# A planner that orders a two-layer hybrid network: new costs, new priority shifts, first hidden blocks transposed on TensorE

## The chip, the cores and the metric

One Trainium2 chip, one NeuronCore of it. The metric is the time of one execution on the device, in microseconds, median of the runs. Engines are named as in the profile: PE is TensorE (PEld its weight loads), DVE is VectorE, ACT is ScalarE, POOL is GpSimd, SP is SyncE, which issues most of the transfers.

## What is computed

256 tokens of width 1024 go through six blocks: a gated feed-forward network (FFN), a hybrid mixer (gated delta rule beside a state-space scan), an FFN, an FFN, a sparse-attention mixer (NSA), an FFN. After each block the residual is scaled, added and layer-normed. All in float32. What matters here:

```
def swiglu(x, w_in, w_out):
    gate, up = jnp.split(x @ w_in, 2, axis=-1)
    return (jax.nn.silu(gate) * up) @ w_out          # D_MODEL 1024, D_FF 2816

proj = x @ w_in                                       # hybrid mixer: 1024 -> 5664 columns
o_a, o_b = gdn_branch(...), ssd_branch(...)           # 64-token chunks with a triangular solve; 128-token chunks
return jnp.concatenate([o_a, o_b], axis=-1) @ w_out

proj = x @ w_in                                       # NSA: 16 heads, compressed + selected + window attention
return o @ w_out
```

## The kernel before

**Numbers.** TensorE's full-rate float32 type rounds its operands, so every operand is split in two: `hi` is a rounded copy (`whi<-raw`, mostly on ACT) and `lo` is the rest (`wlo<-raw,whi`, a subtraction on DVE). A product is hi·hi + hi·lo + lo·hi, three matmuls (`mm3`, `split`). So each 512 KB tile of weights (`raw`, 128x1024) costs one transfer, one ACT instruction and one DVE instruction before its matmuls.

**FFN blocks.** The 2816 hidden columns are 22 blocks of 128 (`ffn`, L1274 on). In FFN 2, 3 and 4 the first four blocks are made by `small(b)` (L1339) for each half b of 128 tokens, tokens on partitions: matmuls into a `ps` bank, silu on ACT, product on DVE (`sg`). The second matmul needs them with hidden columns on partitions, so they are turned. `S_TURN` (L117) says how, one entry for each FFN and half: 0 is four PE transposes into an `mp` bank (`mp<-ident,sg`), read from there by `split`; 1 is `turn` (L793): ACT takes the float words apart (`words<-sg`), SP issues a transposing transfer (`turned<-words`), ACT puts the words together (`gT<-turned`). FFN 1 does not use `S_TURN`. The other blocks come in groups of four by a seven-product scheme (`wide`, L945) with sums of weight tiles on DVE (`raw<-raw,raw`) or by POOL transfers that add (POOLq `raw<-in_ffn_w_in_dram`), or singly (`ordinary`). `term` adds each finished block into four `acc` banks.

**Banks.** PSUM has 2 banks under the name `ps`, 2 under `mp` and 4 under `acc` (`CAPS`). `mp` takes the transposes of layer norm, of `small` with S_TURN 0, and products of `wide`.

**The order of work.** Nothing is emitted as written. `K` records every instruction with its dependencies in a `Plan`; `Plan.order` (L481) then runs a list scheduler over five engines. An instruction's priority is its place in the program plus a shift from the table `SHIFTS` (L51): for each block and engine, runs of (count, shift). `price` (L396) says what an instruction costs, `LAT` what a hand-over between two engines costs, and `Rings` (L259) when a transfer lands, from two queues (SP and POOL) that share the bandwidth. What comes out is a fixed order for each engine, and each engine keeps to it: an instruction that waits holds up all behind it on its engine. All emission goes through one line, so every row of the profile has L682; rows are told apart by tiles.

Of the kernel before, what the change touches and what calls it, by code (L numbers as in the profile page):

```python
# [43 lines left out]

SHARE = {"tensor": 1.0}

# [6 lines left out]
        "tensor": [(54, 312), (4, 0), (5, 633), (69, 0), (5, -34), (66, 1525), (75, 578)],  # L53
        "vector": [(26, 0), (10, -363), (1, 0), (2, -172), (4, 0), (16, -136), (12, 0), (1, 159), (9, 0), (1, 199), (1, 0), (8, 70), (3, 121),
            (29, 0), (70, -36)],
        "scalar": [(100, 156), (13, 0), (2, 210)],
        "sync": [(8, 0), (2, -433), (2, -185), (1, -325), (1, 0), (2, -185)],
    },
    1: {
        "tensor": [(78, 97), (43, 0), (2, -396), (28, 0), (3, 84), (20, -93), (49, 2), (3, -168), (50, 0), (1, 71), (63, 0), (1, 591), (16, 0),  # L60
# [4 lines left out]
        "vector": [(63, 0), (21, -37), (19, 176), (54, 0), (2, 370), (17, 0), (1, 364), (31, 0), (3, 471), (18, 144), (7, 0), (6, -279), (2, 382),  # L65
            (51, -379), (5, 136), (68, 0), (23, -449)],
        "scalar": [(73, 0), (3, -1527), (2, 92), (36, 0), (1, 444), (84, 0), (25, -178), (5, 174), (5, 0), (1, 92)],
    },
    2: {
        "tensor": [(43, 277), (1, 0), (3, 89), (43, 0), (8, 217), (14, 0), (2, 189), (26, 0), (1, -988), (266, 0), (1, 1556), (4, 0), (2, 1846),  # L70
            (84, 1283), (37, 0), (5, 1492), (7, 1066), (51, 661), (9, 306), (69, 0), (74, -484), (25, 0), (3, -165)],
        "vector": [(37, 382), (25, 303), (16, 0), (1, 336), (10, 0), (1, 407), (25, 0), (2, 1164), (2, 0), (4, 853), (2, 0), (1, 880), (4, 16),
            (6, 0), (6, 1372), (30, 0), (8, 391)],
        "scalar": [(120, 177)],
    },
    3: {
        "tensor": [(54, 860), (19, 0), (2, 765), (29, 432), (13, 0), (13, 277), (2, 424), (29, 0), (4, 114), (9, 402), (2, 590), (53, 0), (7, 303),
            (1, 264), (126, 0), (6, 1322), (23, 959), (31, 445), (221, 32), (120, 0), (24, 459)],
        "vector": [(8, 0), (81, 492), (1, -170), (2, 0), (95, -215)],
        "scalar": [(35, 0), (1, 556), (71, 0), (7, -444)],  # L80
    },
    4: {
        "tensor": [(37, 330), (25, 0), (9, -331), (233, 0), (131, -65), (2, 141), (14, 0), (6, 80), (28, 0), (4, 349)],
        "vector": [(25, 0), (1, 42), (42, 0), (3, -385), (71, 0), (1, -281), (7, 0), (1, -271)],
        "scalar": [(91, 0), (8, -135), (27, 0), (2, -179), (11, 0), (2, 344), (70, 0), (1, -358), (2, -304), (3, 108)],
        "gpsimd": [(64, 67)],
        "sync": [(2, 0), (41, -12)],
    },
    5: {
        "tensor": [(113, 0), (14, 265), (47, 0), (15, -122), (47, 239), (12, 0), (108, 365), (12, 0), (8, -4893), (69, 0), (10, 46), (8, 0),  # L90
            (11, 181), (7, 0), (3, 239), (4, 0), (15, 405), (31, 0), (2, 110), (24, 0), (1, 292), (41, 0), (179, -266)],
        "vector": [(21, 0), (26, -366), (83, 0), (1, -97), (3, 0), (3, -70), (47, -356)],
        "scalar": [(43, 0), (7, -108), (64, -148), (17, 226)],
# [23 lines left out]
S_TURN = (0, 1, 1, 1, 0, 1, 0, 1)  # L117
# [136 lines left out]
class Op:  # L254
    __slots__ = ("eng", "fn", "args", "kw", "idx", "prio", "cost", "table", "deps", "succ", "ndep", "ready", "start",
                 "end", "alloc", "dense", "alts", "tiles", "nbytes", "quad", "port", "banks", "pad")


class Rings:  # L259


    LEAD = dict(sync=1500.0, gpsimd=2200.0)
    TAIL = dict(sync=1600.0, gpsimd=4300.0)
    START = 20000.0
    SHARE = dict(sync=0.52, gpsimd=0.48)
# [5 lines left out]
    def advance(self, to):  # L271
        while self.now < to:
            open_ = [e for e in self.left if self.left[e]]
            if not open_:
                self.now = to
                return
            rate = {e: self.SHARE[e] if len(open_) > 1 else 1.0 for e in open_}
            step = min([to - self.now] + [self.left[e][0] / rate[e] for e in open_])
            for e in open_:
                self.left[e][0] -= rate[e] * step  # L280
                if self.left[e][0] < 1e-6:
                    self.left[e].pop(0)
            self.now += step if step > 1e-9 else 1e-9

    def landing(self, eng, at, nbytes, row):
        if eng == "gpsimd":
            work = nbytes / 217.0
        else:
            work = max(150.0, nbytes / (359.0 if row >= 4096 else 341.0 if row >= 2048 else 310.0 if row >= 1024 else
                                        267.0 if row >= 512 else 200.0))  # L290
        if at < self.START:
            work *= 1.07
        at += self.LEAD[eng]
        self.advance(at)
        self.left[eng].append(work)
        other = "sync" if eng == "gpsimd" else "gpsimd"
        mine, more = sum(self.left[eng]), sum(self.left[other])
        a, b = self.SHARE[eng], self.SHARE[other]
        took = mine / a if mine / a <= more / b else more + mine
        return max(self.now, at) + took + (600.0 if at < self.START else self.TAIL[eng])  # L300


class Plan:
# [5 lines left out]
           "vector": dict(tensor=202.0, vector=127.0, scalar=165.0, gpsimd=155.0, sync=120.0),  # L309
           "scalar": dict(tensor=217.0, vector=152.0, scalar=131.0, gpsimd=170.0, sync=150.0),  # L310
           "gpsimd": dict(tensor=203.0, vector=100.0, scalar=150.0, gpsimd=112.0, sync=150.0)}
# [84 lines left out]
    def price(self, op, eng, fn, args, kw):  # L396
# [15 lines left out]
        if fn in DMAS:  # L412
            return 455.0 if eng == "sync" else 1300.0
# [4 lines left out]
        if eng == "scalar":  # L418
            rows = args[0].p1 - args[0].p0

            more = 0
# [55 lines left out]
    TURN = 150.0  # L477
    TABLES = {"Exp": "exp", "Silu": "silu", "Sin": "silu"}


    def order(self, caps):  # L481
        ops = self.ops
        for op in ops:
# [4 lines left out]
            op.ready = 0.0  # L488
            for d in op.deps:
                ops[d].succ.append(op)  # L490
# [35 lines left out]
        def try_alloc(key):  # L526
            q = queues[key]
            while heads[key] < len(q):
# [18 lines left out]
                for op in wait:  # L547
                    op.alloc.remove(t)
                    op.ready = max(op.ready, t.slot_free)
                    if not op.alloc:  # L550
                        release_ready(op)
# [9 lines left out]
        def deps_done(op):  # L561
            for t in list(op.alloc or []):
                if t.slot_free is not None:
                    op.alloc.remove(t)
                    op.ready = max(op.ready, t.slot_free)
            if op.alloc:
# [10 lines left out]
        while left:  # L577
# [42 lines left out]
            if eng == "tensor":  # L620
                partial = op.quad
                l, r = args[1:3]
# [13 lines left out]
            if fn in DMAS:  # L636

                v = args[0] if isinstance(args[0], V) else args[1]
                op.end = rings.landing(e, st, op.nbytes, 256 if fn != "dma_start" else 4 * v.shape[-1])
                free[e] = st + c  # L640
# [8 lines left out]
            for s in op.succ:  # L649
                lat = (620.0 if s.eng == "gpsimd" and s.fn == "dma_start" else 80.0) if fn in DMAS else self.latency(op, eng, s.eng) + (0.0 if eng == "tensor" else s.pad)  # L650
                s.ready = max(s.ready, op.end + lat)
                s.ndep -= 1
# [1898 lines left out]
```

## Time and profile before

| what | value |
|---|---|
| median of 3 runs (lowest, highest) | 1077.56 us (1076.8, 1080.67) |
| the profiled execution | 1073.77 us |
| its span, first to last instruction | 1072.1 us |
| granted TensorE clock, mean over the span | 0.994 |
| PE busy | 1049.2 us, 98% |
| DVE busy | 1006.0 us, 94% |
| ACT busy | 773.7 us, 72% |
| POOL busy | 87.5 us, 8% |
| DMA, mean | 219 GB/s |

Busy time of PE counts a matmul from its issue to the modelled end of its pipeline, and matmuls overlap. So PE can be "busy" and still not at its pace: the pace is the distance between starts. Along the blocks: FFN 1 runs to about 190 us, the hybrid mixer to 420, FFN 2 to 600, FFN 3 to 780, NSA to 895, FFN 4 to the end.

### The profile page before, as it was taken

To read this page: it belongs to the slowest core of one execution; us is meant where nothing else is said; L and a number is where in the kernel's file an instruction comes from. 1 tells how busy PE (TensorE), PEld (TensorE's weight loads), DVE (VectorE), ACT (ScalarE), POOL (GpSimd) and SP (SyncE) were. 2 spreads that over 40 slices of the span, in tenths; PEclk is the share of its full clock that TensorE was granted. 3 is DMA by queue.
4 is the path that set the end of the run, shared out by engine and by line. 5 is a ranking of instruction groups with operands and counts; after the bars stand their busy time and mean duration, and the time that the engine had idled before them with its cause. 6 is when DMAs were issued, how large, how long until landed. Compare 5 with 4: busy or idle time off the path is not lost. (4 is left out here: it accounts for less than half of the span.)

```text
span 1072.1 us, 15945 instructions
## 1 busy us (share of the span) xinstructions
PE 1049.2 (98%) x5698; PEld 868.7 (81%) x5698; DVE 1006.0 (94%) x1413; ACT 773.7 (72%) x1158; POOL 87.5 (8%) x136
## 2 busy tenths in 40 slices
PE   9999999999999999999999999999999999999997
PEld 7877788898889877888878887788887778888886
DVE  7998999898998989899999999999988989999997
ACT  7666876479866966778767486797566975878790
POOL 1001000001000111010000200000021101000100
PEclk9999999999999999999999999999999999999999
DMA  9888996745772689799879857788744346498991
GB/s 328 279 251 267 272 282 202 220 115 148 175 207 71 196 272 302 199 270 286 258 212 312 221 164 232 225 290 239 257 149 172 101 156 177 134 271 236 285 282 40
DMA packets 182809, 234.56 MB, mean 219 GB/s; under 512 B 51197, under 2 KB 112330, under 8 KB 182730
## 3 DMA queue, kind: packets, MB, share of 16 engines
q1 hardware_dynamic: 173482, 215.72, 63.8%
q0 software_dynamic: 9248, 17.83, 9.5%
q8 instruction: 45, 0.74, 0.3%
q14 instruction: 34, 0.28, 0.1%
HBM read 221.30 MB, written 1.07 MB: 207 GB/s over the span
## 5 line engine op out<-in xcount | busy, mean ns | idle before, releaser
L682 DVE TENSOR_TENSOR wlo<-raw,whi 128x1024 fp32r<-128x1024 f32 (+2 forms) x447 | 522.4, 1208 | 9.2 <-ACT whi L682 9.0
L682 ACT ACTIVATE whi<-raw 128x1024 fp32r<-128x1024 f32 (+2 forms) x430 | 426.8, 1044 | 69.9 <-DVE raw L682 51.4
L682 PE MATMUL ps<-whi,x 128*128 128x512 f32 (+1 forms) x544 | 143.6, 384 | 0.0
L682 DVE TENSOR_TENSOR raw<-raw,raw 128x1024 f32<-128x1024 f32 x94 | 112.2, 1219 | 4.7 <-DMA raw<-in_ffn_w_in_dram 4.5
L682 PEld LDWEIGHTS ps<-whi,x 128*128 128x128 f32 x544 | 97.9, 188 | 17.9 <-ACT vg L682 0.2
L682 PE MATMUL ps<-x,whi 128*128 128x256 f32 (+2 forms) x464 | 105.0, 342 | 0.1
L682 PE MATMUL acc<-wlo,gh 128*128 128x512 f32 x253 | 99.0, 391 | 0.1
L682 PE MATMUL acc<-whi,gl 128*128 128x512 f32 x253 | 98.0, 391 | 0.0
L682 PE MATMUL acc<-whi,gh 128*128 128x512 f32 x253 | 96.8, 392 | 0.0
L682 PEld LDWEIGHTS ps<-x,whi 128*128 128x128 f32 (+1 forms) x464 | 77.7, 188 | 10.1 <-ACT cv L682 0.6
L682 PE MATMUL acc<-whi,x 128*128 128x512 f32 x256 | 82.5, 403 | 2.8 <-ACT x L682 1.2
L682 PE MATMUL mp<-whi,x 128*128 128x512 f32 x288 | 78.6, 395 | 0.3 <-ACT vg L682 0.3
L682 PE MATMUL ps<-wlo,x 128*128 128x512 f32 (+1 forms) x272 | 77.8, 383 | 0.6 <-DVE wlo L682 0.6
L682 PE MATMUL mp<-whi,fhi 128*128 128x512 f32 x192 | 75.6, 394 | 0.0
L682 PE MATMUL mp<-whi,flo 128*128 128x512 f32 x192 | 75.4, 393 | 0.0
L682 POOL DMA_DIRECT2D raw<-in_ffn_w_in_dram x34 | 41.1, 1219 | 347.2 <-PE mp L682 171.1
L682 PE MATMUL ps<-x,wlo 128*128 128x256 f32 (+1 forms) x344 | 67.6, 286 | 0.0
L682 PEld LDWEIGHTS mp<-whi,x 128*128 128x128 f32 x288 | 53.9, 190 | 12.9 <-ACT vg L682 1.1
L682 PE MATMUL acc<-whi,g 128*128 128x512 f32 x192 | 63.3, 390 | 0.0
L682 PE MATMUL mp<-wlo,fhi 128*128 128x512 f32 x192 | 60.3, 394 | 2.8 <-DVE wlo L682 2.6
L682 PEld LDWEIGHTS acc<-whi,x 128*128 128x128 f32 x256 | 47.2, 188 | 14.7 <-DVE x L682 2.3
L682 PEld LDWEIGHTS ps<-wlo,x 128*128 128x128 f32 x272 | 49.2, 188 | 9.7 <-DVE wlo L682 1.1
(330 smaller groups left out, 1853.6 us busy)
## 6 DMA issues: line engine op xcount, KB each, us to landing
raw<-in_ffn_w_in_dram SPq DMA_DIRECT2D x162, 512.0 KB, 6.0
raw<-in_ffn_w_out_dram SPq DMA_DIRECT2D x88, 512.0 KB, 5.9
raw<-in_hyb_w_in_dram SPq DMA_DIRECT2D x44, 512.0 KB, 5.3
raw<-in_ffn_w_in_dram POOLq DMA_DIRECT2D x34, 512.0 KB, 8.4
raw<-in_ffn_w_in_dram SPq DMA_DIRECT2D x52, 256.0 KB, 4.4
raw<-in_hyb_w_out_dram SPq DMA_DIRECT2D x16, 512.0 KB, 4.6
raw<-in_nsa_w_in_dram SPq DMA_DIRECT2D x10, 512.0 KB, 5.3
raw<-in_nsa_cmp_w_dram SPq DMA_DIRECT2D x8, 512.0 KB, 3.9
```

Source lines behind the costliest of these rows:

```text
L682: r = getattr(getattr(nc, eng), fn)(*[res(a) for a in args], **{k: res(a) for k, a in kw.items()})
```

## The change

1. `S_TURN` becomes all 0: four halves (both of FFN 2, the second of FFN 3 and of FFN 4) leave the transposing transfer and take the PE transposes.
2. The planner's costs change: issue of a transposing transfer on SP 1350 instead of 455 ns, of any other 500; a weight load that finds no cover adds up to 109 ns to a matmul; hand-overs to PE get shorter (so that this is not counted twice); a transposing transfer that meets one of POOL's costs 1500 ns more; bandwidths, lead and tail of a landing are new; SP stands still when its queue is deep.
3. Every entry of `SHIFTS` is new (more runs per engine; tables for SP in blocks where there were none).

```diff
-S_TURN = (0, 1, 1, 1, 0, 1, 0, 1)
+S_TURN = (0, 0, 0, 0, 0, 0, 0, 0)
 class Rings:
-    LEAD = dict(sync=1500.0, gpsimd=2200.0)
-    TAIL = dict(sync=1600.0, gpsimd=4300.0)
+    LEAD = dict(sync=1400.0, gpsimd=2570.0)
+    TAIL = dict(sync=2000.0, gpsimd=3300.0)
-    SHARE = dict(sync=0.52, gpsimd=0.48)
+    SHARE = dict(sync=0.43, gpsimd=0.57)
+    CLASH = 1500.0
+    DEEP = 9200.0
...
+        if (turning and self.left[other]) or (eng == "gpsimd" and any(t for _, t in self.left[other])):
+            work += self.CLASH
...
-           "vector": dict(tensor=202.0, vector=127.0, scalar=165.0, gpsimd=155.0, sync=120.0),
-           "scalar": dict(tensor=217.0, vector=152.0, scalar=131.0, gpsimd=170.0, sync=150.0),
+           "vector": dict(tensor=140.0, vector=127.0, scalar=165.0, gpsimd=155.0, sync=120.0),
+           "scalar": dict(tensor=155.0, vector=152.0, scalar=131.0, gpsimd=170.0, sync=150.0),
...
-            return 455.0 if eng == "sync" else 1300.0
+            return 1300.0 if eng == "gpsimd" else 500.0 if fn == "dma_start" else 1350.0
...
+                slack = free[e] - op.rel
+                if slack < self.LOAD:
+                    c += min(self.LOAD, self.LOAD - slack)
+                elif 200.0 <= slack < 240.0:
+                    c += 60.0
...
-                free[e] = st + c
+                free[e] = st + c + (max(0.0, rings.deep - rings.DEEP) if e == "sync" else 0.0)
...
 SHIFTS = {
     0: {
-        "tensor": [(54, 312), (4, 0), (5, 633), (69, 0), (5, -34), (66, 1525), (75, 578)],
+        "tensor": [(73, 35), (42, 0), (3, -303), (2, 677), (60, 285), (4, 0), (6, 272), (80, 180), (61, 0), (1, 89), (2, 0), (5, 76), (12, 0),
...
```

In numbers of instructions: PE gets 16 transposes more (`mp<-ident,sg` 16 to 32, one row of the profile each). ACT loses 4 `words<-sg`, 4 `gT<-turned`, and gets 2 more table loads (15 to 17); SP loses 4 transposing transfers (36 to 32); 8 pairs `g<-gT` become `g<-mp`. Copies that may run on either engine are dealt anew: DVE gets 4 `whi<-raw` more (16 to 20) and gives 4 `PT<-mp` to ACT; 8 small products go from POOL to DVE. All else is the same work in another order.

**PE near 100 us (FFN 1).** The two transposes `mp<-ident,vg` and `mp<-ident,su` turn a finished group of four blocks; both use the two `mp` banks. Before:

```order
228 L682 MATMUL mp_198_1159<-ident_7_285,vg_129_836 128x128 x4
229 L682 MATMUL acc_112_778<-wlo_181_1084,g_94_680 128x512
230 L682 MATMUL acc_112_778<-whi_178_1069,g_94_680 128x512
231 L682 MATMUL acc_114_784<-whi_178_1069,g_94_680 128x512
232 L682 MATMUL acc_114_784<-wlo_181_1084,g_94_680 128x512
233 L682 MATMUL acc_114_784<-whi_178_1069,g_94_680 128x512
234 L682 MATMUL acc_118_795<-whi_178_1069,g_94_680 128x512
235 L682 MATMUL acc_118_795<-wlo_181_1084,g_94_680 128x512
236 L682 MATMUL acc_118_795<-whi_178_1069,g_94_680 128x512
237 L682 MATMUL mp_207_1189<-ident_7_285,su_102_729 128x128 x4
```

Now:

```order
238 L707 MATMUL acc_101_707<-whi_171_1031,g_113_773 128x512
239 L707 MATMUL acc_101_707<-wlo_180_1068,g_113_773 128x512
240 L707 MATMUL acc_101_707<-whi_171_1031,g_113_773 128x512
241 L707 MATMUL acc_101_707<-whi_175_1048,g_113_773 128x512
242 L707 MATMUL acc_101_707<-wlo_182_1078,g_113_773 128x512
243 L707 MATMUL acc_101_707<-whi_175_1048,g_113_773 128x512
244 L707 MATMUL acc_114_776<-whi_203_1175,gh_205_1184 128x512
245 L707 MATMUL acc_114_776<-wlo_206_1188,gh_205_1184 128x512
246 L707 MATMUL acc_116_784<-whi_203_1175,gh_205_1184 128x512
247 L707 MATMUL acc_116_784<-wlo_206_1188,gh_205_1184 128x512
248 L707 MATMUL mp_212_1208<-ident_7_284,su_90_653 128x128 x4
```

The `vg` transposes are row 234 now, so 13 matmuls (rows 235 to 247) stand between the two, where 8 stood.

**DVE near 541 us (FFN 2).** `raw<-raw,raw` adds weight tiles that have just landed; `wlo<-raw,whi`, `su` and `vg` work on what is there already. Before:

```order
684 L682 TENSOR_TENSOR wlo_1020_5639<-raw_991_5533,whi_1015_5624 128x1024
685 L682 TENSOR_TENSOR wlo_1023_5649<-raw_994_5544,whi_1019_5637 128x1024
686 L682 TENSOR_TENSOR raw_1010_5610<-raw_1010_5610,raw_1013_5616 128x1024
687 L682 TENSOR_TENSOR wlo_1027_5668<-raw_1002_5574,whi_1025_5658 128x1024
688 L682 TENSOR_TENSOR raw_1012_5614<-raw_1012_5614,raw_1014_5618 128x1024
689 L682 TENSOR_TENSOR su_980_5494<-mp_968_5423,su_980_5494 128x512
690 L682 TENSOR_TENSOR wlo_1031_5691<-raw_1005_5585,whi_1028_5675 128x1024
```

Now:

```order
691 L707 TENSOR_TENSOR wlo_1015_5626<-raw_989_5518,whi_1011_5606 128x1024
692 L707 TENSOR_TENSOR wlo_1020_5641<-raw_993_5531,whi_1014_5623 128x1024
693 L707 TENSOR_TENSOR su_984_5502<-mp_974_5461,su_984_5502 128x512
694 L707 TENSOR_TENSOR wlo_1025_5658<-raw_995_5540,whi_1019_5639 128x1024
695 L707 TENSOR_TENSOR vg_980_5487<-vg_980_5487,su_984_5502 128x512
696 L707 TENSOR_TENSOR wlo_1029_5675<-raw_998_5551,whi_1023_5650 128x1024
697 L707 TENSOR_TENSOR wlo_1032_5687<-raw_1002_5566,whi_1026_5661 128x1024
698 L707 TENSOR_TENSOR wlo_1034_5697<-raw_1005_5577,whi_1031_5680 128x1024
699 L707 TENSOR_TENSOR raw_1010_5601<-raw_1010_5601,raw_1017_5630 128x1024
```

Row 686 of before is row 699 now: six instructions that stood behind it (`su`, `vg` and four `wlo`) stand ahead of it.

**PE at the start of FFN 2.** `mp<-ident,sg` are the transposes that came in; `ps_782`, `ps_807` and `ps_822` are banks in which other products are summed meanwhile. Now (before, no transposes stood in this stretch of matmuls):

```order
1271 L707 MATMUL ps_807_4671<-whi_757_4433,x_780_4537 128x512 x2
1272 L707 MATMUL ps_782_4549<-wlo_801_4635,x_780_4537 128x512
1273 L707 MATMUL ps_782_4549<-wlo_804_4649,x_780_4537 128x512 x2
1274 L707 MATMUL mp_809_4685<-ident_7_284,sg_799_4624 128x128 x2
1275 L707 MATMUL ps_807_4671<-whi_757_4433,x_780_4537 128x512 x2
1276 L707 MATMUL ps_807_4671<-whi_770_4485,x_780_4537 128x512 x4
1277 L707 MATMUL ps_807_4671<-whi_772_4494,x_780_4537 128x512
1278 L707 MATMUL mp_814_4705<-ident_7_284,sg_811_4690 128x128 x2
1279 L707 MATMUL ps_807_4671<-whi_772_4494,x_780_4537 128x512 x3
```

Two transposes each stand between matmuls of another bank. Elsewhere, near 380 us: on SP the last `G<-rates` transfer of the hybrid mixer moves ahead of two of the `w_out` loads that stood before it; on PE the eight matmuls `mp<-xdt,G` that use it stand 9 matmuls earlier (a place in the order 2075, was 2084). Near 805 us (NSA): `PT<-mp`, a copy out of an `mp` bank, is on ACT right after the softmax; it was on DVE behind ten other instructions.

## Rows read from the trace of the kernel before

**Rows 1.** The page, part 1 (busy time of each engine, share of the span, instructions) and part 2 (PE's granted clock in 40 slices, tenths):

```profile
PE 1049.2 (98%) x5698; PEld 868.7 (81%) x5698; DVE 1006.0 (94%) x1413; ACT 773.7 (72%) x1158; POOL 87.5 (8%) x136
...
PEclk9999999999999999999999999999999999999999
```

**Rows 2.** The busy time of the engines in stretches of 20 us (stretch, length, then PE, PEld, DVE, ACT, POOL busy, granted clock, DMA share, GB/s):

```profile
60.00:80.00 20.00, 17.69 (x72) 13.85 (x71) 17.38 (x18) 11.79 (x13) 2.39 (x2) 0.93 0.79 222
...
480.00:500.00 20.00, 20.00 (x90) 16.27 (x89) 20.00 (x19) 18.24 (x21) 0.00 (x0) 1.00 0.99 311
```

**Rows 3.** PE's own waits (engine and tile that waited, on whom, us in total, times, longest), the first four and the last of 15 rows that sum to 14.8 us:

```profile
PE mp L682 <- DVE wlo L682: 2.6, 2, 2.3
PE mp L682 <- DVE G L682: 1.9, 1, 1.9
PE mp L682 <- DVE PT L682: 1.5, 1, 1.5
PE mp L682 <- DVE gl L682: 1.5, 1, 1.5
...
PE mp L682 <- DVE y L682: 0.2, 1, 0.2
```

**Rows 4.** Groups of PE instructions by tile and shape (count | busy us, mean ns of one | idle before, releasers):

```profile
L682 PE MATMUL ps<-whi,x 128*128 128x512 f32 x480 | 133.4, 395 | 0.0
L682 PE MATMUL acc<-whi,x 128*128 128x512 f32 x256 | 82.5, 403 | 2.8 <-ACT x L682 1.2 <-ACT whi L682 1.0 <-DVE x L682 0.6
L682 PE MATMUL acc<-whi,g 128*128 128x512 f32 x192 | 63.3, 390 | 0.0
L682 PE MATMUL ps<-x,whi 128*128 128x512 f32 x224 | 61.0, 403 | 0.1
L682 PE MATMUL acc<-wlo,x 128*128 128x512 f32 x128 | 48.4, 401 | 0.0
L682 PE MATMUL mp<-ident,sg 128*128 128x128 f32 x16 | 2.6, 272 | 0.0
```

**Rows 5.** Timeline (start us, length us, engine, instruction, [idle before <- what ended it]): four matmuls of 512 columns, and four transposes of `sg`, on PE at full pace:

```profile
620.06 1.09 PE L682 MATMUL mp<-whi,x 128*128 128x512 f32 x4
...
618.35 0.60 PE L682 MATMUL mp<-ident,sg 128*128 128x128 f32 x4
```

**Rows 6.** What the transposing path costs its engines: groups on ACT (count | busy, mean ns), and the transfer's issue on SP (count: ns min/median/max):

```profile
L682 ACT ACTIVATE words<-sg 128x1024 uint16<-128x1024 uint16 x4 | 4.2, 1052 | 2.6 <-DVE sg L682 2.6
...
L682 ACT ACTIVATE gT<-turned 128x1024 uint16<-128x1024 uint16 x24 | 32.9, 1369 | 4.0 <-DMA turned<-words 4.0
L682 ACT ACT_TABLE_LOAD x15 | 19.2, 1283 | 1.0 <-PEq L2538 0.8
...
L682 SPq DMA_TRANSPOSE turned<-words x36: 1231/1239/5765, 100.7 to 1016.9; - x36
```

**Rows 7.** Timeline of the waits that this text follows, in order of time:

```profile
98.16 1.06 ACT L682 ACTIVATE whi<-raw 128x1024 fp32r<-128x1024 f32 x1 [1.70 <-DMA raw<-in_ffn_w_out_dram]
...
100.48 0.66 PE L682 MATMUL mp<-ident,su 128*128 128x128 f32 x4 [1.47 <-DVE gl L682]
...
375.98 4.27 SPq L682 DMA_DIRECT2D raw<-in_hyb_w_out_dram  x3
381.90 0.33 SPq L682 DMA_DIRECT2D G<-rates  x1
...
389.31 2.45 ACT L682 ACTIVATE G<-G,arena 128x128 f32<-128x128 f32 x8 [3.48 <-DMA G<-rates]
...
394.93 0.29 PE L682 MATMUL mp<-xdt,G 128*128 128x64 f32 x1 [1.88 <-DVE G L682]
...
412.52 0.50 PE L682 MATMUL acc<-whi,x 128*128 128x512 f32 x1 [1.15 <-ACT x L682]
...
414.31 0.73 PE L682 MATMUL acc<-whi,x 128*128 128x512 f32 x2 [0.60 <-DVE x L682]
...
542.07 1.23 DVE L682 TENSOR_TENSOR raw<-raw,raw 128x1024 f32<-128x1024 f32 x1 [1.86 <-DMA raw<-in_ffn_w_in_dram]
...
547.36 0.74 PE L682 MATMUL ps<-wlo,x 128*128 128x512 f32 x2 [0.63 <-DVE wlo L682]
...
550.78 0.50 PE L682 MATMUL ps<-whi,fhi 128*128 128x512 f32 x1 [0.59 <-ACT whi L682]
...
805.63 0.55 PE L682 MATMUL mp<-ident,P 128*128 128x128 f32 x3 [1.52 <-DVE PT L682]
```

**Rows 8.** Timeline of waits whose surroundings stay as they are or get no more room (72 to 78 us, and 665 us):

```profile
72.91 2.36 DVE L682 TENSOR_TENSOR raw<-raw,raw 128x1024 f32<-128x1024 f32 x2 [2.45 <-DMA raw<-in_ffn_w_in_dram]
...
76.46 0.73 PE L682 MATMUL mp<-wlo,fhi 128*128 128x512 f32 x2 [2.31 <-DVE wlo L682]
...
77.72 0.63 PE L682 MATMUL mp<-whi,fhi 128*128 128x512 f32 x1
78.14 0.63 PE L682 MATMUL mp<-whi,flo 128*128 128x512 f32 x1
...
665.01 0.50 PE L682 MATMUL acc<-wlo,g 128*128 128x512 f32 x1 [0.87 <-DVE wlo L682]
```

**Rows 9.** How long an `mp` bank is held after a pair of transposes of `sg` (600 to 660 us; instruction, count: ns min/median/max, first and last start):

```profile
L682 ACT ACTIVATE g<-mp x2: 377/384/391, 618.8 to 619.1; 128x256 fp32r<-128x256 f32 x2
L682 DVE TENSOR_TENSOR g<-mp,g x2: 415/416/417, 619.3 to 619.6; 128x256 fp32r<-128x256 f32 x2
```

More of the change, by code (lines that the diff above doesn't have):

```diff
@@ L69 @@
-    2: {
[L70 to L74, printed above, removed]
-    },
@@ L277, in advance, with landing @@
             rate = {e: self.SHARE[e] if len(open_) > 1 else 1.0 for e in open_}
-            step = min([to - self.now] + [self.left[e][0] / rate[e] for e in open_])
+            step = min([to - self.now] + [self.left[e][0][0] / rate[e] for e in open_])
             for e in open_:
-                self.left[e][0] -= rate[e] * step
-                if self.left[e][0] < 1e-6:
+                self.left[e][0][0] -= rate[e] * step
+                if self.left[e][0][0] < 1e-6:
                     self.left[e].pop(0)
             self.now += step if step > 1e-9 else 1e-9
-    def landing(self, eng, at, nbytes, row):
+    def landing(self, eng, at, nbytes, row, turning):
         if eng == "gpsimd":
-            work = nbytes / 217.0
+            work = nbytes / 224.0
         else:
[L289 to L292, printed above, removed]
+            work = max(185.0, nbytes / (365.0 if row >= 4096 else 330.0 if row >= 2048 else 305.0 if row >= 1024 else
+                                        281.0 if row >= 512 else 225.0))
+        early = at < self.START
         at += self.LEAD[eng]
         self.advance(at)
-        self.left[eng].append(work)
         other = "sync" if eng == "gpsimd" else "gpsimd"
-        mine, more = sum(self.left[eng]), sum(self.left[other])
+        if (turning and self.left[other]) or (eng == "gpsimd" and any(t for _, t in self.left[other])):
+            work += self.CLASH
+        self.left[eng].append([work, turning])
+        mine, more = sum(w for w, _ in self.left[eng]), sum(w for w, _ in self.left[other])
         a, b = self.SHARE[eng], self.SHARE[other]
         took = mine / a if mine / a <= more / b else more + mine
-        return max(self.now, at) + took + (600.0 if at < self.START else self.TAIL[eng])
+        self.deep = mine
+        return max(self.now, at) + took + self.TAIL[eng]
 class Plan:
@@ L477 @@
     TURN = 150.0
+    LOAD = 109.0
     TABLES = {"Exp": "exp", "Silu": "silu", "Sin": "silu"}
@@ L488, in order @@
             op.ready = 0.0
+            op.rel = -1e9
             for d in op.deps:
@@ L565, in deps_done @@
                     op.ready = max(op.ready, t.slot_free)
+                    op.rel = max(op.rel, t.slot_free)
             if op.alloc:
@@ L638, in order @@
                 v = args[0] if isinstance(args[0], V) else args[1]
-                op.end = rings.landing(e, st, op.nbytes, 256 if fn != "dma_start" else 4 * v.shape[-1])
-                free[e] = st + c
+                op.end = rings.landing(e, st, op.nbytes, 256 if fn != "dma_start" else 4 * v.shape[-1], fn != "dma_start")
+                free[e] = st + c + (max(0.0, rings.deep - rings.DEEP) if e == "sync" else 0.0)
             else:
@@ L651, in order @@
                 s.ready = max(s.ready, op.end + lat)
+                if eng != "tensor":
+                    s.rel = max(s.rel, op.end + lat)
                 s.ndep -= 1
```

62 lines of the change are left out of this document (39 added, 23 removed), and 8 rows, old and new, of the table SHIFTS.

## The prediction

> **What bounds the kernel now.** I read the page's busy shares first. PE is busy for 98% of the span at a granted clock of nearly full speed in every slice, DVE for 94%, ACT for 72% [rows 1]. In an FFN stretch (480 to 500 us) PE and DVE both fill 20.00 of 20 us [rows 2]. So I looked next at what PE waits for: 15 rows that sum to 14.8 us of 1072.1, the largest 2.6 us [rows 3]. The reader is to see that PE hardly ever stands idle for long: over 98% of the span is made of instructions one behind the other, and nothing that only relieves another engine can shorten it. A change of order can take time from three places alone: PE's listed waits; the small excess between neighbours, which the waits do not list; and the work itself.
>
> The small excess shows in the means by group. A matmul of 512 columns reads 390 ns where nothing disturbs it (`acc<-whi,g`), and four in a row take 1.09 us, so their starts lie (1.09 − 0.39)/3 = 0.23 us apart [rows 4, 5]. Other groups of the same shape read 395 to 403 ns. The records of neighbours overlap; the difference to 390 is the part that waited for weights or for a bank.
>
> **Work added and removed.** PE gets 16 transposes. Four take 0.60 us and one record reads 272 ns, so each behind another costs (0.60 − 0.27)/3 = 0.11 us, and 16 cost 1.8 us [rows 4, 5]. They stand in pairs between matmuls of other banks, where the next one starts as it would have; if each stood alone they would cost 16 × 0.272 = 4.4 us. I take 1.8, since the order shows them in pairs, and keep 4.4 as the upper bound.
> The Trainium skill ("TensorE: Matmul & The Clock Gate", Part 4: PE-mode transpose) gives about 275 ns for a 128×128 transpose in one kernel's context; by it the estimate would be 16 × 275 ns = 4.4 us and the whole sum 2.6 us longer. The trace agrees on the length of one record (272 ns) and not on the pace of several.
>
> The transposing path that goes takes from ACT four `words` of 1.05 us and four `gT` of 1.37 us, and adds two table loads of 1.28 us: 9.7 − 2.6 = 7.1 us less. From SP it takes four issues of 1.24 us [rows 6]. ACT is busy for 72% [rows 1], and no listed wait of PE hangs on these, so both count nothing; they are covered by PE's own work of about 98%. If that cover were gone, the most they could give is their length, which I do not add. Eight pairs `g<-gT` become `g<-mp`, one ACT and one DVE instruction as before, 0.38 and 0.42 us [rows 9]; DVE gets four copies more and gives four away. Nothing is counted for these: DVE's work stays within 1 us of its 1006, and it has 66 us of idle time over the span [rows 1].
>
> **Waits that lose their cause.** I followed each long wait of PE to its root [rows 7] and looked where the instructions stand now.
> - 100.48, 1.47 us: ACT waited 1.70 us for a `w_out` load, was late with the product that DVE needed, and PE had only 8 matmuls to cover. Now 13 stand there: 5 × 0.23 = 1.2 us more cover. I credit 1.2.
> - 394.93, 1.88 us: ACT waited 3.48 us for the transfer `G<-rates`, which SP issued at 381.90, behind three `w_out` loads that took 4.27 us to issue. It now goes ahead of two of them, about two thirds of 4.27 us earlier (2.8 us). But PE needs it 9 matmuls, or 2.1 us, earlier. The gain to be had lies between 0 and 1.88; since its issue moves by more than its use, and the transfer has less ahead of it on the queue, I take all 1.88.
> - 414.31, 0.60 us: five `wlo` stood in front of the layer norm's DVE steps and are behind them now. Credit 0.6. The 1.15 us at 412.52 belong to a transfer that landed late, and stay.
> - 547.36 and 550.78, 0.63 and 0.59 us: DVE stood 1.86 us at 542.07 for a tile that had not landed, with `su` and four `wlo` ready behind it. Six ready instructions stand ahead of it now. At the 1.2 us of one such instruction that is far more than 1.86 us. Credit 1.2.
> - 805.63, 1.52 us: the copy `PT` stood on DVE behind ten others; it is on ACT right after the softmax. Credit 1.5.
>
> Together 1.2 + 1.9 + 0.6 + 1.2 + 1.5 = 6.4 us. Bounds: nothing, if each gap comes back somewhere else; 11.0 us, if every wait shown goes (these 6.4, the rest of 100.48, 412.52, and the two of [rows 8]).
>
> **Kept.** The wait at 76.46, 2.31 us, comes from DVE standing 2.45 us for a transfer; the order of these loads and of DVE around it is as before. Behind it matmuls of 0.63 us start 0.42 us apart, at half the clock [rows 8], where 0.23 is usual: some eight of them lose 8 × 0.19 = 1.5 us, and the granted clock of that stretch is 0.93 [rows 2]. This can go only with the wait, so I count it at nothing and keep 1.5 us for the lower bound. At 665.01 the cover shrinks by about 1.4 us; the 0.87 us stay.
>
> **The small excess.** The planner now charges up to 109 ns for a weight load without cover, so it will choose neighbours that cover it. What there is to gain, against 390 ns: 13 × 256 + 13 × 224 + 5 × 480 + 11 × 128 ns = 3.3 + 2.9 + 2.4 + 1.4 = 10.0 us [rows 4]. Between 0 and 10.0 I take a third, 3.3 us: the list scheduler can only choose among what is ready, and the priorities bind it first.
>
> **The sum.** The profiled execution took 1073.8 us. 1073.8 + 1.8 − 6.4 − 3.3 = 1065.9. The median of the three runs is 1077.56, so the profiled execution stands 3.8 us below it; on the median's scale the forecast is 1065.9 + 3.8 = 1069.7, say 1070 us. Lowest: all waits, the clock and all excess go, and only the transposes are added: 1073.8 + 1.8 − 11.0 − 1.5 − 10.0 + 3.8 = 1057. Highest, with the mechanism as I see it but nothing credited and the transposes dear: 1073.8 + 4.4 + 3.8 = 1082.
>
> **The rivals.** What a measurement of this kernel can tell from no change is about 0.5%, 5.4 us.
> - *More goes than I credit.* The loads of FFN 2, 3 and 4 stand some 4 us of PE's work earlier relative to their use in the new order, so also transfers that I left alone may land in time. For: most roots above are transfers that landed late, and their times are what the planner was corrected in. Against: at 480 to 500 us the transfer engines are already 99% taken at 311 GB/s [rows 2], and an earlier issue does not land earlier there. Time: 1056 to 1062.
> - *The waits only change places.* Six blocks in a new order have hundreds of new hand-overs, and none shown by the old trace says that those are met. For: DVE too is full in FFN stretches [rows 2], so what PE gains it would soon wait for there; the order cannot then beat the 20 us of DVE. Against: PE's waits on DVE come to a few us in all [rows 3]. The order would not do what it says, and only the transposes remain: 1077.6 + 1.8 = 1079.4.
> The Trainium skill ("Perfetto Trace Analysis", Identifying the Most-Contended Engine) has TensorE's headroom judged by its weight loads' busy share rather than its matmuls'. By that PE is at 81% here and DVE, at 94%, is the engine to relieve; as the change relieves DVE of nothing, this rival would be the result. The waits in the trace speak against it: an engine that bounds would be waited for by more than 14.8 us.
> - *Slower: the two `mp` banks get scarce.* Each new pair of transposes takes an `mp` bank until DVE has read it. From 618.35, when the transposes begin, to 619.3 + 0.42 = 619.7, when the first pair is read, is 1.4 us [rows 5, 9]. Products of the seven-product scheme and the transposes of the layer norm want the same two banks. If PE has less than 1.4 us of other ready work at each of the eight, it stands for 8 × 1.4 = 11.2 us: 1077.6 + 1.8 + 11.2 = 1090.6. It decides from about 0.5 us of work per pair downwards (8 × 0.9 = 7.2 us). Against it: at the start of FFN 2 the order has seven matmuls of another bank, 1.6 us, between the first two pairs.
>
> **How the numbers follow.** The forecast has a chance of 0.50; its spread, 1062 to 1077, puts 0.36 below 1072.2 and 0.14 above. The larger gain has 0.17, all faster. Waits that change places have 0.20, 0.17 of it within 0.5% and 0.03 beyond. The scarce banks have 0.13, beyond. So faster is 0.36 + 0.17 = 0.53, same 0.14 + 0.17 = 0.31, slower 0.03 + 0.13 = 0.16. The range 1056 to 1083 holds the first three cases and leaves out the scarce banks and a little at each end. The likeliest case's own range, 1062 to 1077, is nearly all at or below the time before.
>
> **What the profile after would show.** Right: `mp<-ident,sg` x32 at about 272 ns with no idle time before it; PE's waits summing to some 8 to 9 us; none of 1 us or more before the transposes of `su` near 100 us, before `mp<-xdt,G`, before the matmuls fed by `raw<-raw,raw` near 545 us, or before the transposes of `P` in NSA; `acc<-whi,x` and `ps<-x,whi` below 400 ns; the wait near 76 us still there. Wrong: the same sum of waits at other tiles (waits that change places); idle time before `mp` tiles on ACT's or DVE's `g` (scarce banks); DVE waiting for `raw` longer than before; or a time below 1062 with the group means unchanged, which would mean that I misjudged where PE loses time.

## The result, and the profile after

The changed kernel takes **1069.6 us** (median of 8 runs, 1066.65 to 1073.53); the kernel before took 1076.44 us (8 runs). The ratio is 0.9935, 95% interval [0.9912, 0.9958]. The forecast was 1070 us. In a second comparison the ratio was 0.9921 [0.9900, 0.9943]. The profiled execution took 1069.88 us, its span is 1068.2 us, 3.9 us less than the span before.

The page, part 1, to be held against [rows 1]:

```profile
PE 1051.2 (98%) x5714; PEld 869.8 (81%) x5714; DVE 1004.6 (94%) x1417; ACT 765.7 (72%) x1154; POOL 88.5 (8%) x130
```

PE has its 16 instructions more and is as full as before, ACT lost 8 us of work, and the time fell by less than 1%. The shares of busy time say nothing of the gain. PE's own waits do (on whom, us in total, times, longest), all of them, against the 14.8 us in [rows 3]:

```profile
PE acc L707 <- ACT whi L707: 2.6, 2, 1.5
PE mp L707 <- DVE wlo L707: 1.8, 2, 1.4
PE acc L707 <- DVE wlo L707: 1.7, 2, 0.9
PE acc L707 <- POOL ones L707: 1.1, 1, 1.1
PE acc L707 <- issue: 0.6, 1, 0.6
PE mp L707 <- ACT P L707: 0.6, 2, 0.3
PE ps L707 <- ACT cv L707: 0.5, 2, 0.2
PE mp L707 <- DVE arena L707: 0.4, 1, 0.4
PE mp L707 <- DVE h L707: 0.2, 1, 0.2
```

They sum to 9.5 us; 8 to 9 were forecast. `G`, `PT`, `gl`, `x` and the two `ps` waits for weights have left the list. The timeline of PE shows the place near 100 us and what is left (start, length, instruction, [idle before <- what ended it]):

```profile
76.64 0.73 PE L707 MATMUL mp<-wlo,fhi 128*128 128x512 f32 x2 [1.38 <-DVE wlo L707]
...
96.60 0.60 PE L707 MATMUL mp<-ident,vg 128*128 128x128 f32 x4
...
100.04 0.60 PE L707 MATMUL mp<-ident,su 128*128 128x128 f32 x4
...
798.23 0.66 PE L707 MATMUL mp<-ident,P 128*128 128x128 f32 x4 [0.36 <-DVE arena L707]
...
1021.72 0.50 PE L707 MATMUL acc<-whi,gh 128*128 128x512 f32 x1 [1.51 <-ACT whi L707]
1022.98 0.50 PE L707 MATMUL acc<-wlo,gh 128*128 128x512 f32 x1 [0.76 <-DVE wlo L707]
...
1029.71 0.50 PE L707 MATMUL acc<-wlo,gh 128*128 128x512 f32 x1 [0.94 <-DVE wlo L707]
```

Before `su` there is no idle time now. The three waits in FFN 4 are new, 3.2 us together. In this trace they lead back to ACT and SP (SPq is SP's issue of transfers):

```profile
1002.30 9.73 SPq L707 DMA_TRANSPOSE turned<-words  x2
1012.13 11.56 SPq L707 DMA_DIRECT2D raw<-in_ffn_w_out_dram  x10
...
1020.62 1.06 ACT L707 ACTIVATE whi<-raw 128x1024 fp32r<-128x1024 f32 x1 [3.06 <-DMA raw<-in_ffn_w_out_dram]
```

Two transposing transfers took 9.73 us to issue, so the `w_out` loads behind them were issued from 1012.13 on, and ACT stood 3.06 us for the first. Each of the 32 such transfers takes 1.28 us in the middle case, but up to 6.09 (before 1.24 and 5.77, [rows 6]):

```profile
L707 SPq DMA_TRANSPOSE turned<-words x32: 1232/1284/6093, 95.8 to 1008.5; - x32
```

The groups of PE that answer to [rows 4]:

```profile
L707 PE MATMUL ps<-whi,x 128*128 128x512 f32 x480 | 136.2, 397 | 0.0
...
L707 PE MATMUL acc<-whi,x 128*128 128x512 f32 x256 | 82.2, 404 | 1.1 <-ACT whi L707 1.1
...
L707 PE MATMUL ps<-x,whi 128*128 128x512 f32 x224 | 62.0, 408 | 0.0
...
L707 PE MATMUL acc<-wlo,x 128*128 128x512 f32 x128 | 47.5, 396 | 0.0
...
L707 PE MATMUL mp<-ident,sg 128*128 128x128 f32 x32 | 5.7, 273 | 0.0
```

The 32 transposes have no idle time before them. The means that were to fall did not: 397, 404, 408 against 395, 403, 403; only `acc<-wlo,x` fell, 401 to 396.

### The profile page after: what moved, and what is told of

It reads as the page before. It is cut to its first block, busy times and chain, and to the rows that moved or that the text cites. A ratio compares the mean times of both kernels' runs of the same rounds, so it can differ in the third digit from the quotient of the medians.

```text
span 1068.2 us, 15981 instructions
## 1 busy us (share of the span) xinstructions
PE 1051.2 (98%) x5714; PEld 869.8 (81%) x5714; DVE 1004.6 (94%) x1417; ACT 765.7 (72%) x1154; POOL 88.5 (8%) x130
## 4 chain that ended last, share of the span: by engine, by line
PE 84%; DVE 7%; DMA 4%; ACT 2%; issue 1%; POOL 1%; SPq 0%; DVEq 0%; POOLq 0%; ACTq 0%
PE acc L707 33%; PE ps L707 26%; PE mp L707 25%; DMA raw<-in_ffn_w_in_dram 2%; DVE arena L707 1%; DMA raw<-in_ffn_w_out_dram 1%; DVE h L707 1%; DVE wlo L707 1%; DVE cv L707 1%; POOL arena L707 1%; DVE o L707 1%; ACT P L707 1%; DMA raw<-in_nsa_cmp_w_dram 1%; DVE F L707 0%; ACT sw L707 0%
## 5 line engine op out<-in xcount | busy, mean ns | idle before, releaser
L707 PE MATMUL ps<-whi,x 128*128 128x512 f32 (+1 forms) x544 | 146.0, 385 | 0.0
L707 PE MATMUL ps<-x,whi 128*128 128x512 f32 (+2 forms) x464 | 106.3, 344 | 0.5 <-ACT cv L707 0.5
L707 PEld LDWEIGHTS acc<-wlo,gh 128*128 128x128 f32 x253 | 47.5, 188 | 12.7 <-DVE wlo L707 2.7
```

The costliest lines, as they stand in the source:

```text
L707: r = getattr(getattr(nc, eng), fn)(*[res(a) for a in args], **{k: res(a) for k, a in kw.items()})
```

## The experiments

Medians are of runs on one chip together with the kernel before; ratios are to that. "PE's waits" is the sum of all rows of its list in the experiment's own trace.

**The changed kernel again, for a second trace.** No edit.

> The changed kernel once more, as the partner of the other runs on this chip and for a second trace. Theory: 0.9935 of before, the same waits of PE at the same tiles (sum 8.9 us, the largest near 1021.7 and 76.6 us). Rival, that a part of the 6.9 us lies in waits that come and go from run to run: the sum of PE's waits moves by 2 us or more between the two traces.

Measured: 1067.5 us, ratio 0.9921 [0.9900, 0.9943]. Its profiled execution was its fastest, 1064.08 us. PE's waits:

```profile
PE acc L707 <- ACT whi L707: 1.2, 2, 1.0
...
PE acc L707 <- DVE wlo L707: 0.7, 1, 0.7
...
PE mp L707 <- DVE wlo L707: 0.3, 1, 0.3
```

With the other six rows they sum to 5.5 us, 4 us less than in the first trace: the wait near 76 us was 0.31 instead of 1.38, and the three of FFN 4 had shrunk to one of 0.7. SP and ACT in FFN 4:

```profile
999.37 10.06 SPq L707 DMA_TRANSPOSE turned<-words  x2
1009.53 8.36 SPq L707 DMA_DIRECT2D raw<-in_ffn_w_out_dram  x10
...
1015.12 1.06 ACT L707 ACTIVATE whi<-raw 128x1024 fp32r<-128x1024 f32 x1 [0.17 <-PE ps L707]
```

The two transposing transfers took no less here, 10.06 us, and yet ACT did not wait for the load behind them. So their long issue alone does not make PE wait in FFN 4: the first load was turned into `whi` 5.6 us after its issue began, where the first trace needed 8.5. Why it landed sooner is not shown.

So the rival holds for a part: the waits that hang on a landing come and go, and the 3.9 us between two single traces do not give the gain to better than a few us. The waits credited in the prediction are absent from both traces.

**Four waits of the kernel before taken away by hand.** A table of moves on the finished order; planner, costs and shifts as before.

```diff
+SLOTS = [(3275, 3289)]
+MOVES = [(711, [717, 718, 720, 721, 723, 724, 726, 728, 729, 730]), (3275, [3289]), (3454, [3455]), (6345, [6325, 6334, 6339])]
...
+    for a, b in SLOTS:
+        a, b = order[a][2][0].t, order[b][2][0].t
+        a.slot, b.slot = b.slot, a.slot
+    for first, these in MOVES:
...
+        moved[at:at] = rest
```

> The kernel before in its own order, with four groups of instructions moved by hand and nothing else: near 100 us ten ready matmuls ahead of the transposes of su (wait 1.47 us); near 380 us the transfer G<-rates one w_out load earlier on SP, their buffers exchanged (wait 1.88); near 414 us the layer norm's x ahead of its bn_stats on DVE (0.60); near 805 us PT ahead of three other DVE instructions (1.52). The theory that PE's listed waits are what the change removed: 1.47 + 1.88 + 0.60 + 1.52 = 5.5 us less than before, ratio 0.995, and these four waits gone from the trace. The rival that waits only change places: the same time as before within 2 us, with new waits of PE that sum to about 5 us.

Measured: 1073.95 us, ratio 0.9978 [0.9963, 0.9993], or 2.4 us [0.8, 4.0] less. The two theories share it: PE's waits sum to 12.8 us, 2.0 less than before, and some of them are new. On PE:

```profile
101.49 0.60 PE L682 MATMUL mp<-ident,su 128*128 128x128 f32 x4
...
106.17 1.19 PE L682 MATMUL mp<-whi,x 128*128 128x512 f32 x4 [1.76 <-DVE su L682]
...
805.47 0.63 PE L682 MATMUL mp<-ident,P 128*128 128x128 f32 x4 [1.30 <-DVE arena L682]
```

The wait for `G` (1.88 us) is gone and did not come back. The wait near 100 us is gone from the transposes and stands 4.7 us later, 1.76 us long. Near 414 us the 0.60 us are gone, and 0.34 us stand at 416.1. The one near 805 us is 1.30 instead of 1.52, now for the copy that stands behind `PT`. What happened near 100 us shows on DVE:

```profile
100.29 0.69 DVE L682 TENSOR_TENSOR gl<-mp,gh 128x512 fp32r<-128x512 f32 x1 [1.88 <-ACT gh L682]
100.90 4.62 DVE L682 TENSOR_TENSOR wlo<-raw,whi 128x1024 fp32r<-128x1024 f32 x4
105.44 0.68 DVE L682 TENSOR_TENSOR su<-mp,su 128x512 f32<-128x512 f32 x1
```

PE finished its `mp` bank earlier, but `su<-mp`, which empties it, stands behind four `wlo` on DVE and still ends at 106.1. To give PE more to do ahead of one wait is worth nothing where the next bank hangs on the same queue of DVE; the changed kernel orders DVE anew as well, and there the place has no wait.

**Each new transpose five times.**

```diff
+                sg = fn == "transpose" and args[1].t.name == "sg"
+                for _ in range(4 if sg else 0):
+                    nc.tensor.transpose(*[res(a) for a in args])
```

> The changed kernel in the same order, each of the 32 transposes of sg done five times in a row into the same place: 128 transposes more. If a transpose behind another costs PE its pace of 0.11 us: 128 x 0.11 = 14 us more than the changed kernel. If each costs its record of 0.272 us: 35 us more. If the two mp banks are scarce, the longer hold (0.9 us more for each pair) adds waits of PE before other mp tiles on top of 14 us.

Measured: 1081.62 us, 14.1 us over the changed kernel run beside it. 14.1 / 128 = 0.110 us each; the ratios, 1.0052 [1.0034, 1.0070] and 0.9921 [0.9900, 0.9943], keep it to 11 to 17 us, far from 35. PE's waits sum to 7.9 us, between the two traces of the changed kernel, so the longer hold of the banks added none: the bank rival gets no support from it. The test adds transposes behind transposes only; what it costs PE to go back to other matmuls is not in it.

**Two of the waits that are left, by hand.** In FFN 4 two loads go ahead of the transposing transfers on SP; in FFN 1 one `wlo` goes ahead of a sum that waits for a landing.

```diff
+MOVES = [(528, [540, 525]), (8017, [7984, 8001])]
```

> The changed kernel with two places moved by hand. In FFN 4, on SP, the next two w_out loads go ahead of two transposing transfers, which took 6.09 and 3.54 us to issue at 1002.3 us while these loads stood behind them (PE's waits 1.51, 0.76 and 0.94 us at 1021.7 to 1029.7). In FFN 1, on DVE, a wlo that was ready goes ahead of the sum raw<-raw,raw that waits 1.57 us for a landing (PE's wait 1.38 us at 76.6). Theory, that what is left of PE's waits is again order: 1.51 + 0.76 + 0.94 + 1.38 = 4.6 us less than the changed kernel. Rival: the transposing transfers land later behind two more loads, gT on ACT waits for them, and PE waits there: no gain, or 1 to 3 us lost.

Measured: 1077.47 us, ratio 1.0010 [0.9996, 1.0025]: nearly 10 us slower than the changed kernel. The rival was right, and its price was short. SP, ACT and PE in FFN 4:

```profile
1003.41 1.25 SPq L707 DMA_DIRECT2D raw<-in_ffn_w_out_dram  x2
1004.75 12.54 SPq L707 DMA_TRANSPOSE turned<-words  x2
1017.39 11.08 SPq L707 DMA_DIRECT2D raw<-in_ffn_w_out_dram  x8
...
1021.80 1.34 ACT L707 ACTIVATE gT<-turned 128x1024 uint16<-128x1024 uint16 x1 [4.82 <-DMA turned<-words]
...
1024.10 0.54 PE L707 MATMUL acc<-whi,gh 128*128 128x512 f32 x1 [3.21 <-ACT whi L707]
...
1026.38 0.63 PE L707 MATMUL acc<-whi,gh 128*128 128x512 f32 x1
1026.81 0.63 PE L707 MATMUL acc<-wlo,gh 128*128 128x512 f32 x1
```

With two more loads in front the transposing transfers took 12.54 us instead of 9.73, `gT` held ACT for 4.82 us, and the `whi` behind it came later than before the move. PE stood 3.21 and 0.72 us, and then worked at half its clock: starts 0.43 us apart, 0.83 granted between 1020 and 1040 us.

**The move in FFN 1 alone.**

```diff
+MOVES = [(528, [540, 525])]
```

> The changed kernel with the one move in FFN 1 alone (the wlo that is ready ahead of the sum raw<-raw,raw that waits for a landing), the transposing transfers of FFN 4 left where they are. If the 10 us lost with both moves came from FFN 4: as the changed kernel or up to 1.4 us faster (PE's wait near 76 us), 1066 to 1070 us. If they came from FFN 1: near 1077 us.

Measured: 1068.3 us, ratio 0.9927 [0.9907, 0.9947], the same as the changed kernel. So the loss came with the move in FFN 4. In single traces that block is 3.0 to 6.6 us longer with the move than in the three traces without it; the profiled execution with both moves is the fastest of its twelve, 3.8 us below their median, and where the rest of the 9 to 10 us lies is not shown. The wait near 76 us turns into 0.38 and 0.37 us at 76.5 and 82.3, which no median can tell apart. No version here beats the changed kernel.

**Parts of the change, with the order drawn again.** Four kernels: `S_TURN` as before, with each shift kept on its instruction; the price of uncovered weight loads left out; old shifts and `S_TURN` with new costs; new shifts and `S_TURN` with old costs.

```diff
-S_TURN = (0, 0, 0, 0, 0, 0, 0, 0)
+S_TURN = (0, 1, 1, 1, 0, 1, 0, 1)
```

> The changed kernel with S_TURN as it was before (four halves by the transposing transfer again), new costs and new shifts kept, each shift on the instruction that it was on. As the prediction has it (ACT's and SP's savings are hidden, only PE's 16 transposes count): 1.8 us less than the changed kernel, 1066 to 1068 us. The rival, that a transposing transfer holds up SP and the loads behind it (6.09 and 3.54 us for one issue in the traces of the changed kernel): the four that come back cost 1 to 6 us each where loads stand behind them, so 3 to 12 us more, with PE's waits on whi and wlo at the first blocks of FFN 2, 3 and 4.

Measured: 1091.98 us, ratio 1.0149 [1.0110, 1.0189], PE's waits 24.8 us.

```diff
-    LOAD = 109.0
+    LOAD = 0.0
```

> The changed kernel, where the planner charges nothing for an uncovered weight load (LOAD 0 instead of 109 ns), so that the order is drawn again without it. The prediction's step that this price takes a third of the small excess: the means of acc<-whi,x, ps<-x,whi and ps<-whi,x go up, by about 3.3 us over all, and the time with them. The rival, that the price moves no such neighbours: the means stay as they are (404, 408, 397 ns) within 2 ns; what the time does then comes from other waits.

Measured: 1096.37 us, ratio 1.0175 [1.0141, 1.0209], PE's waits 26.8 us. `ps<-whi,x` and `ps<-x,whi` read 398 and 408 ns, as with the price; `acc<-whi,x` reads 422, with 11.2 us of idle time in front of its group.

```diff
-S_TURN = (0, 0, 0, 0, 0, 0, 0, 0)
+S_TURN = (0, 1, 1, 1, 0, 1, 0, 1)
...
-        "tensor": [(73, 35), (42, 0), (3, -303), (2, 677), (60, 285), (4, 0), (6, 272), (80, 180), (61, 0), (1, 89), (2, 0), (5, 76), (12, 0),
+        "tensor": [(54, 312), (4, 0), (5, 633), (69, 0), (5, -34), (66, 1525), (75, 578)],
...
```

> The shifts and S_TURN of the kernel before under the new costs. If the new landing and issue prices by themselves let the planner see the waits: most of the 6 us that PE's waits lost, so 1070 to 1072 us. If the shifts do it, and shifts fit only the costs they were drawn under: no gain or slower than before, 1077 to 1090 us, with new waits of PE.

Measured: 1117.0 us, ratio 1.0367 [1.0333, 1.0402], PE's waits 38.6 us.

> The shifts and S_TURN of the changed kernel under the old costs. If the shifts carry the gain: near the changed kernel, 1068 to 1072 us. If the costs carry it, or the two fit only together: slower than before, 1077 to 1090 us.

Measured: 1098.78 us, ratio 1.0202 [1.0172, 1.0232], PE's waits 27.5 us. Its edit is the mirror of the last one: only `SHIFTS` and `S_TURN` are new.

All four are slower than the kernel before, by 15 to 40 us, and none by an amount that one of its theories gave alone. Before reading them as the worth of a part, the redrawing itself had to be priced.

**Controls: a cost that is nearly the same.** 100 ns for 109; a lead of 1410 ns for 1400; on the side of before, 1510 for 1500.

```diff
-    LOAD = 109.0
+    LOAD = 100.0
```

> The changed kernel with the price of an uncovered weight load at 100 ns instead of 109, as a control: a cost that is nearly the same, so that only the order is drawn again while the shifts stay. If leaving the price out by itself cost the kernel without it its 27 us, this one stays within 3 us of the changed kernel, 1066 to 1072 us. If the shifts fit one drawing of the order alone, it is slower by 10 to 30 us too, with PE's waits at 20 us and more.

Measured: 1095.16 us, ratio 1.0181 [1.0162, 1.0201], PE's waits 26.2 us. One of them is 9.90 us, and it has nothing to do with weight loads:

```profile
430.59 1.09 PE L707 MATMUL mp<-ident,h 128*128 128x128 f32 x4 [9.90 <-DVE h L707]
```

PE has nothing left between the hybrid mixer and FFN 2 and stands through a layer norm.

```diff
-    LEAD = dict(sync=1400.0, gpsimd=2570.0)
+    LEAD = dict(sync=1410.0, gpsimd=2570.0)
```

> The changed kernel with the lead of a landing from SP at 1410 instead of 1400 ns, a second control: the order stays the same for a longer stretch (on PE up to row 1990). If the shifts fit one drawing alone: slower by 3 to 20 us, all of it after FFN 2 has begun (row 1990 lies near 380 us), with the waits near 76 and 100 us as in the changed kernel. If small changes of cost are harmless: within 2 us of it.

Measured: 1072.78 us, ratio 0.9978 [0.9963, 0.9992], some 5 us over the changed kernel by the ratios. PE's waits 11.2 us. The one for `G` is back, 1.6 us, and one at 428.25 us is new:

```profile
PE mp L707 <- DVE G L707: 1.6, 1, 1.6
...
428.25 0.33 PE L707 MATMUL mp<-ident,sg 128*128 128x128 f32 x1 [1.84 <-DVE sg L707]
```

> The kernel before with the lead of a landing from SP at 1510 instead of 1500 ns, the control for that side. If its shifts too fit one drawing: slower by 2 to 15 us. If not: within 2 us of the kernel before.

Measured: 1077.52 us, ratio 1.0003 [0.9982, 1.0024]: no difference, although the order did change: about 150 of PE's 5698 matmuls have one of another tile in their place (by the same count about 260 of 5714 with the lead of 1410, and 580 with the price of 100). So that its shifts fit one drawing alone is shown for the changed kernel, and not for the kernel before.

So 9 ns in one price cost as much as leaving the price out. The traces of all these kernels, those with moves by hand too, stand side by side, each from one execution (the one with more transposes has more work and is left out):

| kernel | PE's waits, us | span, us |
|---|---|---|
| changed, second trace | 5.5 | 1062.4 |
| changed, move in FFN 1 | 6.9 | 1062.5 |
| changed, two moves | 9.1 | 1072.0 |
| changed, first trace | 9.5 | 1068.2 |
| changed, lead 1410 | 11.2 | 1071.4 |
| before, four moves | 12.8 | 1071.5 |
| before | 14.8 | 1072.1 |
| before, lead 1510 | 15.8 | 1079.7 |
| changed, old `S_TURN` | 24.8 | 1092.8 |
| changed, price 100 | 26.2 | 1093.1 |
| changed, price left out | 26.8 | 1094.9 |
| new shifts, old costs | 27.5 | 1097.0 |
| old shifts, new costs | 38.6 | 1116.8 |

The spans go with the waits, in nearly the same order; the kernel with two moves is the exception, in part for its matmuls at half clock (above), which are no wait. From the first row to the last, 33.1 us of waits go with 54.4 us of span, 1.6 us for each. A part of the rest is the clock: the granted clock, mean over the span, is 0.997 in the first row and 0.984 in the last, by an estimate from these two figures up to 15 us of it. That all of it acted through PE's waits is not shown.

The four kernels above measure how far the shifts are from fitting another drawing of the order, not what turning on PE, the costs or the shifts are worth. What each part gives by itself stays open. The runs show that the new shifts without the new costs, and the new costs without the new shifts, are slower than before, and that the gain belongs to the one order that the new inputs draw together: 10 ns in one cost took some 5 us of it.

## Why the prediction was right, and which step failed

The time, the direction and the size came out as forecast, though not every term of the sum did. Step by step:

- **16 transposes, +1.8 us: right for the transposes, short for what stands behind them.** 0.110 us each by 128 more of them, no idle time before any; the record's 272 ns was the wrong price. But that the next matmul "starts as it would have" is wrong by some 0.7 us, as shown below.
- **Five places, −6.4 us: right in four.** 6.7 us of waits stood there [rows 7], and all of these are gone. In NSA others took their place: instead of the 1.52 us before the transposes of `P` there are 0.27, 0.36 and 0.31 us, in both traces nearly the same, so 0.6 us of the 1.5 was gained. That the causes were read rightly is shown by an experiment for `G` alone (one move, wait gone). For 100 us the reading was short: cover for PE was not enough, DVE's order behind it had to change too.

```profile
792.22 1.06 PE L707 MATMUL mp<-ident,P 128*128 128x128 f32 x8 [0.27 <-ACT P L707]
...
833.50 1.09 PE L707 MATMUL mp<-ident,P 128*128 128x128 f32 x8 [0.31 <-ACT P L707]
```

- **Kept waits: too cautious.** The 1.15 us at 412.52 and the 0.87 us at 665.01 are gone, and the 2.31 us near 76 us, said to stay, became 1.38 and 0.31. The transfers of that stretch did not stay as they were: their share went from 0.79 to 0.98, and the granted clock from 0.93 [rows 2] to 1.00, as this line of the first trace has it:

```profile
60.00:80.00 20.00, 18.62 (x85) 14.92 (x85) 18.43 (x20) 13.47 (x16) 2.39 (x2) 1.00 0.98 276
```

- **New waits at nothing: wrong.** Places that had none before hold 5.2 us of waits in the first trace and 2.5 in the second, 3.2 and 0.7 us of them in the places of FFN 4 shown above. They are the lesser form of the rival in which waits change places.
- **The small excess, −3.3 us: this step failed.** The four means of [rows 4] gave 10.0 us against 390 ns; in the first trace after, (397 − 390) × 480 + (404 − 390) × 256 + (408 − 390) × 224 + (396 − 390) × 128 ns = 11.7 us, in the second 9.8. The mean was misread as something that every record carries. In a group whose mean is 396 to 408 the median record reads 389 to 393; a few are long, and the order on PE shows which:

```profile
793.04 0.48 PE L707 MATMUL ps<-whi,x 128*128 128x512 f32 x1
793.36 0.39 PE L707 MATMUL ps<-wlo,x 128*128 128x512 f32 x1
```

Ahead of the first stand eight transposes, and it takes 0.48 us; the next takes 0.39, and starts 0.32 us after it instead of 0.23. Of the 82 records of 460 to 600 ns in the four groups, 52 follow a transpose `mp<-ident`, ten of them one of `sg`; before there were 74, of which 42 follow a transpose, three of them one of `sg`. The transposes of `sg` stand in 13 groups now and stood in 5; behind each of the 13 the next matmul of 512 columns takes 0.48 us. So the change adds eight such places with its own transposes, 8 × 0.09 = 0.7 us on top of the 1.8 (an estimate from these records), and the price that the planner was given did not take away what stands behind a turn. Eight records of `ps<-x,whi` in the first trace after are longer for another reason: they ran at half clock, near 310 us; before there were four such, near 306 us, and in the second trace none.

**The same by blocks.** This is an estimate from the three traces. Charge each matmul the usual distance to the next start for its shape (0.227 us for 512 columns, 0.109 us for a transpose); that makes 1002.3 us before and 1004.1 us after, the 1.8 us of the transposes apart. What a block takes beyond that is time that PE lost, in listed waits or otherwise. A block ends here where the layer norm's transposes of the second half of the tokens begin.

| block | lost before, us (of it waits) | first trace after | second trace after |
|---|---|---|---|
| FFN 1 | 13.5 (6.1) | 9.9 (3.5) | 8.7 (2.6) |
| hybrid mixer | 19.1 (4.7) | 16.2 (1.1) | 15.1 (1.0) |
| FFN 2 | 3.1 (1.2) | 0.8 (0) | 0.8 (0) |
| FFN 3 | 3.6 (1.2) | 1.1 (0) | 1.1 (0) |
| NSA | 22.3 (1.5) | 22.6 (1.1) | 22.6 (1.1) |
| FFN 4 | 8.2 (0) | 13.5 (3.6) | 10.0 (0.7) |

PE lost 5.6 and 11.4 us less in all, and 5.3 and 9.3 us of that are listed waits: the waits are most of the gain. It was made in the first four blocks. NSA, credited with 1.5 us, gained nothing; FFN 3, credited with nothing, gained 2.5 us; FFN 4 gave back 1.8 to 5.3. What is lost outside the waits fell by 1.1 and 1.3 us in FFN 2 and 3 and rose by 0.8 us in NSA and 1.1 to 1.7 us in FFN 4. Why is not shown.

In sum, on the scale of the profiled execution the forecast was 1073.8 − 7.9. The first trace after is 3.9 us shorter in span, the second 9.7, and the medians lie 6.8 us apart (9.4 us in the second comparison). The terms of the two: waits −5.3 and −9.3, transposes +1.8 in both, means +1.7 and −0.2; that leaves −2.1 in the first and −2.0 in the second for what is in no term, the half clock near 76 us, 1.5 us by the prediction's own sum, among it. The 3.3 us that the excess did not give came from waits and clock that the prediction had kept: the direction and the main mechanism, waits that go, were right, but that the sum met the time to within 1 us is luck, by terms that made up for each other.

Of the rivals, the scarce banks did not come: the five-fold transposes kept the banks longer and added no wait. The larger gain, 1056 to 1062 us, was reached by no run; the fastest took 1064.08. Waits that change places are real (the hand moves show two, FFN 4 has three), but in the changed kernel they took back 5.2 and 2.5 us, by the two traces, of the 10.5 and 11.8 us that went elsewhere.

The Trainium skill ("Perfetto Trace Analysis", Identifying the Most-Contended Engine) has TensorE's headroom judged by its weight loads, 81% here, and would have had DVE relieved. The trace disagrees as to the whole: DVE's work changed by 1.4 us of 1006 and the kernel got faster. Near 100 us, in the kernel with four moves, DVE did set when PE could go on, but by the order of its queue (four `wlo`, 4.62 us, ahead of `su`) and not by its total of work.

## What to carry to other kernels

Where one engine is full, list its waits one by one, follow each to its root, and credit only those whose cause the new order takes away; here such a list met a gain of 0.6%, with some luck: a second trace of the same kernel moved its sum by 4 us. Look at a group's mean only after its distribution: a mean 3% above the floor may be a tenth of the records, most of them behind one kind of neighbour. And do not ablate a tuned scheduler by changing one of its inputs: the control with nearly the same input is part of the experiment.

## What was not expected of the hardware

The issue of a transposing transfer, 1.28 us in the middle case of the first trace after, took 6.09 us at 1002.3 us, behind four loads that had been issued on the same queue since 998.3 us; with six loads ahead two of them took 12.54 us, and what stands behind them on SP is issued that much later. Loads ahead are not the whole condition: at 399.95 us, in the same trace, one took 1.25 us behind six loads issued since 395.1 us. What else it takes is open.

After PE had stood for 3.21 and 0.72 us, twelve matmuls took 0.63 us each and started 0.43 us apart instead of 0.23, the lower of its two clock levels (1.2 of 2.4 GHz): 12 × 0.20 = 2.4 us on top of the waits. A matmul of 512 columns right behind a transpose took 0.48 us instead of 0.39 and held up the next by 0.09. And two executions of one program differed by 4 us in PE's waits, at places where a transfer lands late.
